# Forming weight low parts by an accumulating DMA in the mLSTM, and turning its last head inside the preceding way down

## The chip, the cores and the metric

The kernel runs on one core of one Trainium2 chip. The metric is the time of one execution on the device, in microseconds; the figure for a kernel is the median of its runs. The core has five engines that run side by side and meet only at semaphores: PE (matrix products), DVE (VectorE), ACT (ScalarE), POOL (GpSimd) and SP, which here only issues DMAs. DMAs issued by SP, ACT and POOL are carried out by the same 16 DMA engines.

## The reference, cut to what matters

Two layers of a streaming encoder over 512 frames of width 1024. Each layer is a half-step SwiGLU FFN, a mixer, a second FFN and a gated embedding, each with a layer norm behind it. The mixer of the first layer is an mLSTM with four heads, and the change lies in it:

```python
def mlstm_mixer(x, w_in, b_in, conv_w, norm_g, w_out):
    proj = x @ w_in + b_in
    qk, v, z, gates = jnp.split(proj, [...], axis=-1)
    qk = jax.nn.silu(causal_depthwise_conv(qk, conv_w))
    ...
    h = mlstm_cell(q, k, v, ig, fg)          # chunked matrix memory, 4 heads of 512 values
    mu = jnp.mean(h, axis=-1, keepdims=True)
    var = jnp.mean(jnp.square(h - mu), axis=-1, keepdims=True)
    h = ((h - mu) * lax.rsqrt(var + LN_EPS)).reshape(B, S, ML_INNER) * norm_g
    h = (h * jax.nn.sigmoid(z)).astype(x.dtype)
    return h @ w_out
```

## The kernel before, in words

All products are float32 built from three products of a narrower type: every operand is split into a high part (the value rounded to that type) and a low part (what the rounding left out), and `mm3` (L252 to L254) adds high times high, high times low and low times high.

**Weights.** The class `Weights` streams all weights through two stages. SP loads 1 MB pieces into a ring of three raw buffers (`wraw`); each gives two tiles of 128x1024. `fill` turns a raw tile into `whi` by a copy on ACT (L182) and `wlo` by a subtraction (L183) on DVE, or on POOL where the caller passes `low=pool`. In the mLSTM there are six tiles of split weights: four of kind "main" and two of kind "extra". A tile is freed by `release`, which fills the next tile of the fixed list `order` if a buffer of that tile's kind is free. With `later=True` the buffer is held until `refill` (which always subtracts on DVE).

**One head.** For each head h the list holds 4 tiles for q and k, 4 for v, 4 for z, and 4 rows of the output weights of the head before. The program order of a head is: `project_qk` (4 groups of 24 matmuls; each group's tile is then released with `low=pool`), `project_v`, `scores`, z blocks 0 and 1, `mix` (the head's values and their norm; a chain of small DVE and POOL operations per block of 128 frames, ending in `hn`), `refill(4)`, z blocks 2 and 3 (released with `low=pool`), and then `down(prev)`: the way down of the head before, 4 blocks of frames t, each 4 row groups k times 6 matmuls (`dps<-whi,hh`, `dps<-wlo,hh`, `dps<-whi,hl`). In the last block each k releases its tile. Then `gate_turn` turns the head's own result: 16 transposes on PE (`hps`, L964), a product with the gate `sz` on DVE (`hzf`, L967), and a split into `hh` on ACT and `hl` on DVE. The next head's way down uses them. After head 3 a last `down` follows at once, with the norm and the transposes of x (`xps`) for the next FFN inside it.

Which kinds the list gives matters at one place: in the way down of head 2, the releases of k = 0 and 1 fill nothing (the next tile is of the other kind), k = 2 fills one tile and k = 3 fills three. The first two of these four are the third and fourth row groups of the last way down, the other two belong to the next FFN.

Each engine works through its instructions in the order written; there is no scheduler.

Of the kernel before, what the change touches and what calls it, by code (L numbers as in the profile page):

```python
# [9 lines left out]
F32 = mybir.dt.float32  # L10
F32R = mybir.dt.float32r
AF = mybir.ActivationFunctionType
OP = mybir.AluOpType
# [3 lines left out]
P = 128  # L17
D = 1024
KB = D // P
SEQ = 512  # L20
TB = SEQ // P
# [3 lines left out]
HEADS = 4  # L25
# [20 lines left out]
class Weights:  # L46
# [112 lines left out]
    def fill(self, most=1000, low=None):  # L159
        while most and self.next_split < len(self.order):  # L160
            kind, js, make = self.order[self.next_split]
            if not self.free.get(kind):
                return
            for j in js or ():
                while j not in self.raws:
                    if not self.load(self.loads[j][1]):
                        return
            shape = [P, 2, 512]
            if js is not None:
                src, used = make()  # L170
                shape = list(src.shape)
            hi = self.pools[kind].tile(shape, F32R, name="whi", tag="whi")
            lo = self.pools[kind].tile(shape, F32R, name="wlo", tag="wlo")
            self.free[kind] -= 1
            self.next_split += 1
            if js is None:
                make(hi, lo)
                continue
            parts = 2 if self.next_split == 1 else 1
            for i in range(parts):  # L180
                s = slice(i * shape[1] // parts, (i + 1) * shape[1] // parts)
                self.nc.scalar.activation(hi[:, s], src[:, s], AF.Copy)  # L182
                (low or self.nc.vector).tensor_sub(lo[:, s], src[:, s], hi[:, s].bitcast(F32))  # L183
            self.ready.append((kind, (hi, lo)))
            most -= 1
            for j in used:
                self.left[j] -= 1
            while self.load():
                pass
# [32 lines left out]
def hybrid_trunk(ctx: ExitStack, tc, x, p, ln_g, ln_b, ffn1_wgu, ffn1_wd, ffn2_wgu, ffn2_wd,  # L222
# [25 lines left out]
    vec, sca, pool = nc.vector, nc.scalar, nc.gpsimd  # L248
# [286 lines left out]
        hooks.extend([lambda: turn_x(TB - 2, halves=(0,)), lambda: turn_x(TB - 2, halves=(1,)),  # L535
                      lambda: turn_x(TB - 1, halves=(0,)), last_turn])

    def down(hs, first, norm=None, low=None):

        n = len(hs)  # L540
        ws, kinds = [], []
        for t in range(TB):
            banks = [dn_bank("dps"), dn_bank("dps")]
            for k in range(n):
                if k == len(ws):
                    ws.append(W.take())
                    kinds.append(W.kind)
                if norm is not None and k in (1, 2) and t >= 2:
                    turn_x(t - 2, up_bank, (k - 1,))
                if norm is not None and k == 1 and t:  # L550
                    norm.apply(t - 1)
                st = [a[:, t * P:(t + 1) * P] for a in hs[k]]
                for half, ps in enumerate(banks):
                    mv = [a[:, 0, half * 512:(half + 1) * 512] for a in ws[k]]
                    mm3(ps, st, mv, k == 0, k == n - 1)
                if t == TB - 1:
                    kind = "rows" if kinds[k] == "rows" else None
                    if norm is None:
                        W.release(kind=kind, low=low)
                    elif kind == "rows":  # L560
                        W.free[kind] += 1
                    else:
                        W.release(later=bool(W.held), low=pool)
                        if not W.held:
                            W.held.append("none")
            for half, ps in enumerate(banks):
                residual(t, half, ps, first)
                if norm is not None:
                    norm.stats(t, half, 2)
        if norm is not None:  # L570
            norm.apply(TB - 1)
            set_hooks()
# [163 lines left out]
    def mlstm():  # L736
        b_in = ml_b_in
        with stage_pool("extra", EXTRA) as extra, stage_pool("ml_parts") as near, stage_pool("ml") as mp:
# [83 lines left out]
            def big(tag, dt, name):  # L822
                return (near if tag in "AB" else mp).tile([P, 4, SEQ], dt, name=name, tag=tag)

            def project_qk(h):

                qh, ql = big("A", F32R, "qh"), big("B", F32R, "ql")

                def project():
                    ps = up_bank("qps")  # L830
                    up(ps, W.take())
                    return ps

                banks = deque()
                if h == 0:
                    banks.extend(up_staged())
                late = None
                for i in range(4):
                    ps = banks.popleft() if banks else project()
                    ch = (i // 2 * QK + h * DQK) // P + i % 2  # L840
                    pad = tmp.tile([P, SEQ + 4], F32, name="pad", tag="pad", bufs=3)
                    vec.memset(pad[:, 0:3], 0.0)
                    sca.activation(pad[:, 3:3 + SEQ], ps, AF.Identity, bias=col("b_qk", ch))
                    acc = tmp_tile("acc")
                    vec.tensor_scalar(acc, pad[:, 0:SEQ], col("conv", ch), None, op0=OP.mult)
                    for j in range(1, CONV):
                        vec.scalar_tensor_tensor(acc, pad[:, j:j + SEQ], col("conv", j * 16 + ch), acc,
                                                 op0=OP.mult, op1=OP.add)
                    if late is not None:
                        late()  # L850

                    def late(i=i, acc=acc):
                        sca.activation(acc, acc, AF.Silu)
                        split(qh[:, i], ql[:, i], acc)

                    W.release(low=pool)
                    if h == 0 and i == 1:
                        gate_products()
                        banks.append(project())
                    run_hook()  # L860
                    if h == 0 and i == 2:
                        gate_logs()
                late()
                return qh, ql
# [18 lines left out]
            def project_z(h, sz, i):  # L883

                ps = up_bank("zps")
                up(ps, W.take())
                sca.activation(sz[:, i], ps, AF.Sigmoid, bias=col("b_z", h * 4 + i))
                vec.tensor_scalar(sz[:, i], sz[:, i], col("norm_g", h * 4 + i), None, op0=OP.mult)
                W.release(later=i < 2, low=pool)

            def row_tile():
                return mp.tile([P, SEQ], F32, name="rbc", tag="rbc")
# [64 lines left out]
                return hn  # L957

            def gate_turn(h, hn, sz):
                hh, hl = big("hh", F32R, "hh"), big("hl", F32R, "hl")  # L960
                for t in range(TB):
                    ps = (dn_bank if t % 2 else up_bank)("hps").rearrange("p (k c) -> p k c", k=4)
                    for i in range(4):
                        nc.tensor.transpose(ps[:, i], hn[:, t, i * P:(i + 1) * P], ident)  # L964
                    s = slice(t * P, (t + 1) * P)
                    hf = tmp_tile("hzf").rearrange("p (k c) -> p k c", k=4)
                    vec.tensor_mul(hf, ps, sz[:, :, s])  # L967
                    split(hh[:, :, s], hl[:, :, s], hf)
                return [(hh[:, i], hl[:, i]) for i in range(4)]

            prev = None
            for h in range(HEADS):
                vb = mp.tile([P, DV], F32, name="vb", tag="sh0")
                sca.dma_start(vb, row_ap(b_in, 2 * QK + h * DV, DV))
                if h:
                    rt = row_tile()
                    load_row(rt, h)
                qk = project_qk(h)
                if h == 0:
                    rt = row_tile()  # L980
                    v = project_v(h, vb, (None, gate_sums, lambda: (gate_rows(), load_row(rt, h))))
                else:
                    v = project_v(h, vb)
                W.release()
                ss = scores(h, qk, rt)
                sz = big("B", F32, "sz")
                W.release()
                W.release(2, later=True)
                for i in range(2):
                    project_z(h, sz, i)  # L990
                hn = mix(h, ss, v)
                W.refill(4)
                for i in range(2, 4):
                    project_z(h, sz, i)
                if prev is not None:
                    down(prev, h == 1, low=pool)
                else:
                    norm = Norm(0, 1)
                prev = gate_turn(h, hn, sz)
            down(prev, False, norm)  # L1000
            W.close("extra")

# [253 lines left out]
```

## Time and profile before

| | |
|---|---|
| median of 3 runs | 2289.18 us (2288.74 to 2290.45) |
| profiled execution, its own time | 2285.76 us |
| its span, first to last instruction | 2284.0 us |
| mean granted PE clock | 0.997 |
| busy: PE, DVE, ACT, POOL | 2239.8, 1495.8, 784.2, 206.4 us |
| mLSTM, about | 366 to 798 us of the span |

In the profile's rows a group is named by the line in the code, the engine, the operation, and output<-inputs by the names of the tiles; then the shape and the count. A row of the timeline begins with its start and its duration in microseconds; what stands in square brackets behind it is how long the engine was idle before it and which engine's work ended that. A row of the waits gives the sum, the number and the longest. A row of the windows gives, for a stretch, its length, each engine's busy time with the number of instructions, the granted PE clock, the mean share of the DMA engines in use, and GB/s.

### The profile page before, as it was taken

Reading aid. Unit: us, or ns where it says so; the run is one execution under the profiler, and the core shown is the slowest. Engines: PE = TensorE matmul, PEld = TensorE weight load, DVE = VectorE, ACT = ScalarE, POOL = GpSimd, SP = SyncE. Lnnn points to the kernel's source line nnn. Section 1 sums busy time; section 2 is a strip of 40 time slices with the busy share of each in tenths; the row PEclk is TensorE's granted clock in tenths of the full one; section 3 lists DMA queues with packets and bytes.
Section 4 is the critical chain, followed back from the end, with each engine's and each line's share of the span. In section 5 each row is a group of like instructions: output and inputs, shape, how many; then the busy total and the mean of one; then the engine's idle time right before and its main releaser. Section 6 shows DMA issues by size and latency. Waiting matters only on the chain.

```text
span 2284.0 us, 26044 instructions
## 1 busy us (share of the span) xinstructions
PE 2239.8 (98%) x10622; PEld 1873.3 (82%) x10622; DVE 1495.8 (65%) x2093; ACT 784.2 (34%) x1032; POOL 206.4 (9%) x143
## 2 busy tenths in 40 slices
PE   8999999999999999999999999999999999999997
PEld 7888888887878788888878888888888888888886
DVE  4566659676666656666687566668566674666677
ACT  3333333442534123333243233333333332333332
POOL 1000002132232300000010000001021210000010
PEclk9999999999999999999999999999999999999999
DMA  7332222133231333331332333222322243332212
GB/s 232 113 98 86 93 86 95 48 114 110 66 102 56 120 111 120 111 96 62 111 120 88 112 105 111 93 70 95 131 93 86 75 133 113 129 111 83 83 65 74
DMA packets 172848, 228.30 MB, mean 100 GB/s; under 512 B 4788, under 2 KB 130836, under 8 KB 172728
## 3 DMA queue, kind: packets, MB, share of 16 engines
q1 hardware_dynamic: 165824, 211.83, 28.6%
q10 hardware_dynamic: 6616, 14.69, 2.0%
q8 instruction: 83, 1.36, 0.2%
q14 instruction: 37, 0.30, 0.0%
q0 software_dynamic: 288, 0.12, 0.0%
HBM read 224.51 MB, written 2.11 MB: 99 GB/s over the span
## 4 chain that ended last, share of the span: by engine, by line
PE 82%; DVE 12%; issue 2%; POOL 2%; ACT 1%; DMA 1%; POOLq 0%; SPq 0%; ACTq 0%; DVEq 0%
PE fps L253 13%; PE fps L254 13%; PE fps L252 13%; PE gps L253 4%; PE gps L254 4%; PE gps L252 4%; PE dps L253 3%; PE dps L254 3%; PE dps L252 3%; DVE wlo L183 2%; DVE xt L512 2%; DVE st L500 1%; PE gups L252 1%; PE vps L252 1%; PE gups L253 1%
## 5 line engine op out<-in xcount | busy, mean ns | idle before, releaser
L252 PE MATMUL fps<-xh,whi 128*128 128x512 f32 x1312 | 510.6, 389 | 0.0
L253 PE MATMUL fps<-xl,whi 128*128 128x512 f32 x1312 | 510.4, 389 | 0.0
L254 PE MATMUL fps<-xh,wlo 128*128 128x512 f32 x1312 | 510.4, 389 | 0.0
L183 DVE TENSOR_TENSOR wlo<-wraw,whi 128x1024 fp32r<-128x1024 f32 (+1 forms) x274 | 336.0, 1242 | 199.2 <-ACT whi L182 197.4
L182 ACT ACTIVATE whi<-wraw 128x1024 fp32r<-128x1024 f32 (+1 forms) x333 | 344.1, 1048 | 263.3 <-PE dps L254 126.2
L252 PEld LDWEIGHTS fps<-xh,whi 128*128 128x128 f32 x1312 | 246.3, 188 | 51.1
L254 PEld LDWEIGHTS fps<-xh,wlo 128*128 128x128 f32 x1312 | 246.3, 188 | 51.0
L253 PEld LDWEIGHTS fps<-xl,whi 128*128 128x128 f32 x1312 | 246.3, 188 | 50.9
L183 DVE TENSOR_TENSOR wlo<-wquarter,whi 128x1024 fp32r<-128x1024 f32 x112 | 137.2, 1225 | 201.9 <-ACT whi L182 201.9
L182 ACT ACTIVATE whi<-wquarter 128x1024 fp32r<-128x1024 f32 x112 | 118.7, 1059 | 238.0 <-PE gps L254 177.8
L183 POOL TENSOR_TENSOR wlo<-wraw,whi 128x1024 fp32r<-128x1024 f32 x59 | 151.8, 2581 | 278.5 <-ACT whi L182 247.4
L254 PE MATMUL gps<-whi,flo 128*128 128x512 f32 x448 | 174.3, 389 | 0.0
L252 PE MATMUL gps<-whi,fhi 128*128 128x512 f32 x448 | 174.3, 389 | 0.0
L253 PE MATMUL gps<-wlo,fhi 128*128 128x512 f32 x448 | 174.3, 389 | 0.0
L508 POOL TENSOR_TENSOR rs<-rs,eps_pow 128x1 f32<-128x1 f32 x32 | 30.3, 947 | 1542.7 <-DVE rs L507 1538.3
L701 ACT ACTIVATE sg<-fps 128x512 f32<-128x512 f32 x80 | 47.9, 598 | 279.1 <-PE fps L254 279.1
L521 DVE TENSOR_TENSOR xt<-xt,gps 128x512 f32<-128x512 f32 x224 | 143.2, 680 | 0.0
L253 PE MATMUL dps<-wlo,hh 128*128 128x512 f32 x256 | 101.6, 397 | 9.5 <-DVE wlo L183 9.5
L257 ACT ACTIVATE fhi<-h 128x512 fp32r<-128x512 f32 x112 | 69.5, 625 | 116.2 <-DVE h L637 45.8
L252 PE MATMUL dps<-whi,hh 128*128 128x512 f32 x256 | 101.9, 398 | 1.8 <-ACT hh L257 1.8
L254 PE MATMUL dps<-whi,hl 128*128 128x512 f32 x256 | 101.4, 396 | 1.7 <-DVE hl L258 1.7
L258 DVE TENSOR_TENSOR flo<-h,fhi 128x512 fp32r<-128x512 f32 x112 | 75.7, 688 | 36.4 <-ACT fhi L257 36.4
(266 smaller groups left out, 3909.6 us busy)
## 6 DMA issues: line engine op xcount, KB each, us to landing
wraw<-in_ffn_wgu_dram SPq DMA_DIRECT2D x80, 1024.0 KB, 5.3
wquarter<-in_ffn_wd_dram SPq DMA_DIRECT2D x64, 512.0 KB, 3.8
wraw<-in_ml_w_in_dram SPq DMA_DIRECT2D x24, 1024.0 KB, 5.4
wraw<-in_gm_w_in_dram SPq DMA_DIRECT2D x15, 1024.0 KB, 5.8
wraw<-in_ffn_wd_dram SPq DMA_DIRECT2D x12, 1024.0 KB, 5.0
wraw<-in_ml_w_out_dram SPq DMA_DIRECT2D x8, 1024.0 KB, 5.0
wraw<-in_ple_wg_dram SPq DMA_DIRECT2D x8, 1024.0 KB, 5.1
wraw<-in_gm_w_out_dram SPq DMA_DIRECT2D x8, 1024.0 KB, 4.9
```

The costliest lines, as they stand in the source:

```text
L182: self.nc.scalar.activation(hi[:, s], src[:, s], AF.Copy)
L183: (low or self.nc.vector).tensor_sub(lo[:, s], src[:, s], hi[:, s].bitcast(F32))
L252: mm(ps, st[0], mv[0], start=start, stop=False, skip_group_check=more)
L253: mm(ps, st[0], mv[1], start=False, stop=False, skip_group_check=more)
L254: mm(ps, st[1], mv[0], start=False, stop=stop, skip_group_check=more)
L257: sca.activation(hi, src, AF.Copy)
L258: vec.tensor_sub(lo, src, hi.bitcast(F32))
L500: vec.bn_stats(self.st[t][:, i], xt[:, t, i * D // n:(i + 1) * D // n])
L508: pool.tensor_tensor(rs[:, 1:2], rs[:, 0:1], eps_pow, op=OP.pow)
L512: vec.scalar_tensor_tensor(y[:, c], y[:, c], rstd, self.b_bc[:, c], op0=OP.mult, op1=OP.add)
L521: vec.tensor_add(dst, dst, ps)
L701: sca.activation(sg, ps, AF.Silu)
```

## The change

Three edits, all in the mLSTM. First, `fill` knows a third way to form a low part, `low="dma"`: ACT writes the negated, rounded value into `wlo` (a second ACT copy per tile), and a DMA issued by POOL adds the raw tile onto it, from SBUF to SBUF. Second, every place in the mLSTM that passed `low=pool` now passes `"dma"`: 36 tiles in all. Third, `gate_turn` returns a function that turns one block of frames; for heads 0 to 2 all four blocks are turned behind the way down as before, and for head 3 each block is turned inside the way down of head 2, behind that way's block t, into buffers that held `vh` and `vl`.

```diff
@@ Weights.fill
                 self.nc.scalar.activation(hi[:, s], src[:, s], AF.Copy)
-                (low or self.nc.vector).tensor_sub(lo[:, s], src[:, s], hi[:, s].bitcast(F32))
+                if low == "dma":
+                    self.nc.scalar.activation(lo[:, s], src[:, s], AF.Copy, scale=-1.0)
+                    self.nc.gpsimd.dma_start(lo[:, s], src[:, s], accum_op=OP.add)
+                else:
+                    (low or self.nc.vector).tensor_sub(lo[:, s], src[:, s], hi[:, s].bitcast(F32))
@@ down
-    def down(hs, first, norm=None, low=None):
+    def down(hs, first, norm=None, low=(None,) * 4, between=None):
...
-                        W.release(kind=kind, low=low)
+                        W.release(kind=kind, low=low[k])
...
                 residual(t, half, ps, first)
...
+            if between is not None:
+                between(t)
@@ mlstm, project_qk and project_z
-                    W.release(low=pool)
+                    W.release(low="dma")
...
-                W.release(later=i < 2, low=pool)
+                W.release(later=i < 2, low="dma")
@@ gate_turn
-                hh, hl = big("hh", F32R, "hh"), big("hl", F32R, "hl")
-                for t in range(TB):
-                    ps = (dn_bank if t % 2 else up_bank)("hps").rearrange("p (k c) -> p k c", k=4)
+                if h < HEADS - 1:
+                    hh, hl = big("hh", F32R, "hh"), big("hl", F32R, "hl")
+                else:
+                    hh, hl = (near.tile([P, 4, SEQ], F32R, name=n, tag=g) for n, g in (("hh", "vh"), ("hl", "vl")))
+                def turn(t):
+                    ps = (dn_bank if t % 2 and h < HEADS - 1 else up_bank)("hps").rearrange("p (k c) -> p k c", k=4)
...
-                return [(hh[:, i], hl[:, i]) for i in range(4)]
+                return [(hh[:, i], hl[:, i]) for i in range(4)], turn
@@ the loop over heads
+                last = h == HEADS - 1
+                if last:
+                    hs, turn = gate_turn(h, hn, sz)
                 if prev is not None:
-                    down(prev, h == 1, low=pool)
+                    down(prev, h == 1, low=[None, None, "dma", "dma"] if last else ["dma"] * 4,
+                         between=turn if last else None)
...
-                prev = gate_turn(h, hn, sz)
+                if not last:
+                    hs, turn = gate_turn(h, hn, sz)
+                    for t in range(TB):
+                        turn(t)
+                prev = hs
```

What stands on ACT at the way down of head 2 and into the last one (whi and wlo are tiles of split weights, hh the turned result of head 3, xh the turned x for the next FFN). Before:

```order
L182 ACTIVATE whi_6002<-wraw_5822 128x1024
L182 ACTIVATE whi_6012<-wraw_5822 128x1024
L182 ACTIVATE whi_6018<-wraw_5832 128x1024
L182 ACTIVATE whi_6024<-wraw_5896 128x1024
L257 ACTIVATE hh<-hzf 128x4x128 x4
```

And in the changed kernel:

```order
L262 ACTIVATE hh_5930<-hzf_6039 128x4x128
L182 ACTIVATE whi_6063<-wraw_5852 128x1024
L185 ACTIVATE wlo_6064<-wraw_5852 128x1024
L182 ACTIVATE whi_6074<-wraw_5852 128x1024
L185 ACTIVATE wlo_6075<-wraw_5852 128x1024
L182 ACTIVATE whi_6081<-wraw_5862 128x1024
L185 ACTIVATE wlo_6082<-wraw_5862 128x1024
L182 ACTIVATE whi_6088<-wraw_5928 128x1024
L185 ACTIVATE wlo_6089<-wraw_5928 128x1024
L262 ACTIVATE hh_5930<-hzf_6102 128x4x128
```

Each of the four tiles now takes two ACT copies, and three of the four splits of the turned blocks stand ahead of them instead of behind.

What stands on POOL from the end of head 3's `mix` on (hr is the norm of the last blocks). Before:

```order
L952 TENSOR_TENSOR hr<-hr,eps_pow 128x1 x4
L183 TENSOR_TENSOR wlo<-wraw,whi 128x1024 x6
L508 TENSOR_TENSOR rs<-rs,eps_pow 128x1 x2
```

And in the changed kernel:

```order
L959 TENSOR_TENSOR hr_5829<-hr_5829,eps_pow_105 128x1
L186 DMA wlo_5892<-wraw_5659 128x1024
L186 DMA wlo_5924<-wraw_5659 128x1024
L186 DMA wlo_6064<-wraw_5852 128x1024
L186 DMA wlo_6075<-wraw_5852 128x1024
L186 DMA wlo_6082<-wraw_5862 128x1024
L186 DMA wlo_6089<-wraw_5928 128x1024
L513 TENSOR_TENSOR rs_6147<-rs_6147,eps_pow_105 128x1
```

Six subtractions became six issues of a DMA, at the same places in POOL's order.

What stands on PE at the join between the two ways down. Before:

```order
L254 MATMUL dps<-whi,hl 128x512
L964 MATMUL hps<-ident,hn 128x128 x16
L252 MATMUL dps<-whi,hh 128x512
```

And in the changed kernel, where such a group of four stands behind each of the four blocks (the last is shown):

```order
L259 MATMUL dps<-whi,hl 128x512
L977 MATMUL hps<-ident,hn 128x128 x4
L257 MATMUL dps<-whi,hh 128x512
```

Twelve of the sixteen transposes moved ahead, into the way down of head 2; four are left at the join.

## The prediction

> **What bounds the kernel now.** I read the page's first part, then PE's waits, then windows over the ways down of the mLSTM, and last the timeline around each wait.
>
> ```profile
> PE 2239.8 (98%) x10622; PEld 1873.3 (82%) x10622; DVE 1495.8 (65%) x2093; ACT 784.2 (34%) x1032; POOL 206.4 (9%) x143
> PE dps L253 <- DVE wlo L183: 9.5, 6, 1.8
> 533.06:559.48 26.42, 22.93 (x97) 17.83 (x96) 13.14 (x16) 4.82 (x5) 5.26 (x3) 1.00 0.35 120
> 637.60:663.49 25.89, 22.91 (x97) 17.83 (x96) 12.93 (x15) 4.82 (x5) 6.14 (x3) 1.00 0.36 122
> 741.61:767.52 25.91, 22.92 (x98) 17.82 (x97) 12.94 (x15) 2.69 (x3) 3.35 (x2) 1.00 0.28 82
> 767.52:798.10 30.58, 27.94 (x129) 22.47 (x128) 24.96 (x40) 8.71 (x12) 14.98 (x8) 0.94 0.44 155
> 761.42 1.39 DVE L521 TENSOR_TENSOR xt<-xt,dps 128x512 f32<-128x512 f32 x2 [4.21 <-PE dps L254]
> 767.02 1.39 DVE L521 TENSOR_TENSOR xt<-xt,dps 128x512 f32<-128x512 f32 x2 [4.21 <-PE dps L254]
> ```
>
> PE is busy 98% of the span, and the change removes no matmul: it can only win where PE stands still. PE waits for a DVE low part six times, all in the ways down. The four windows are the three ways down inside heads 1 to 3 and the last one. The two residual rows, 5.60 us apart, give the undisturbed pace: one block of 24 matmuls in 5.60, a way down in 22.40, one k of six in 1.40, one matmul in 0.233. The three ways take 78.22 instead of 67.2: 11.0 us lost.
>
> Why DVE is late there:
>
> ```profile
> 530.66 2.40 POOL L183 TENSOR_TENSOR wlo<-wraw,whi 128x1024 fp32r<-128x1024 f32 x1
> 530.73 2.35 DVE L953 TENSOR_TENSOR hr<-hr 128x1 f32<-128x1 f32 x1 [0.73 <-POOL hr L952]
> 534.02 4.54 DVE L183 TENSOR_TENSOR wlo<-wraw,whi 128x1024 fp32r<-128x1024 f32 x2
> 535.02 2.45 POOL L183 TENSOR_TENSOR wlo<-wraw,whi 128x1024 fp32r<-128x1024 f32 x1 [1.97 <-ACT whi L182]
> 533.06 0.39 PE L252 MATMUL dps<-whi,hh 128*128 128x512 f32 x1
> 535.29 0.50 PE L253 MATMUL dps<-wlo,hh 128*128 128x512 f32 x1 [1.84 <-DVE wlo L183]
> 538.61 0.50 PE L253 MATMUL dps<-wlo,hh 128*128 128x512 f32 x1 [1.65 <-DVE wlo L183]
> L953 DVE TENSOR_TENSOR hr<-hr x16: 159/160/2359, 441.3 to 739.0; 128x1 f32<-128x1 f32 x16
> L183 DVE TENSOR_TENSOR wlo<-wraw,whi x274: 681/1224/3418, 7.9 to 2237.2; 128x1024 fp32r<-128x1024 f32 x136, 128x512 fp32r<-128x512 f32 x1
> ```
>
> A DVE operation on one column, median 0.16 us, takes 2.35 and ends with POOL's subtraction; the next pair takes 4.54 instead of 2 times 1.22 beside another. While POOL subtracts, DVE stands. The two hits are 2.2 and 2.1 us, and PE's two waits follow.
>
> **The change, part by part.** *POOL's 36 subtractions go.* Without the first hit the first low part is there at 535.29 − 2.2 = 533.1; PE wants it one matmul after 533.06, at 533.29. Without both, the second is there at 538.61 − 4.3 = 534.3, wanted 1.40 after the first, at 534.7. Both waits go, by 0.2 and 0.4 us. Taken over three heads: 11.0 gained. The DMA that replaces the first subtraction is issued at the same moment, and I know one row for an issue of as many pieces (1024):
>
> ```profile
> 5.18 0.95 POOL L469 DMA_DIRECT2D graw<-in_ml_w_in_dram  x1
> ```
>
> DVE was idle there, so whether an issue holds DVE is not shown. If it does, DVE loses 0.8 of the 2.2 us, 0.6 past its margin, in three heads: 9.2 is the lower end, 11.0 the upper. I take 11.0, since the page shows DVE held by arithmetic of POOL alone.
>
> *The last head's turn moves.* Now PE stands behind the 16 transposes:
>
> ```profile
> 767.52 1.91 PE L964 MATMUL hps<-ident,hn 128*128 128x128 f32 x16
> 771.24 0.50 PE L252 MATMUL dps<-whi,hh 128*128 128x512 f32 x1 [1.82 <-ACT hh L257]
> 772.80 0.70 PE L254 MATMUL dps<-whi,hl 128*128 128x512 f32 x1 [0.82 <-DVE hl L258]
> 769.40:772.90 3.50, 0.86 (x4) 0.40 (x3) 1.68 (x2) 1.79 (x3) 3.50 (x3) 1.00 0.00 0
> 772.90:776.30 3.40, 3.40 (x9) 2.66 (x10) 2.54 (x3) 0.76 (x2) 3.40 (x2) 0.50 0.88 284
> 766.32 1.06 ACT L182 ACTIVATE whi<-wraw 128x1024 fp32r<-128x1024 f32 x1 [22.88 <-PE dps L254]
> ```
>
> It waits 1.82 and 0.82, and after that thin stretch the granted clock is 0.50 for 3.40 us, which costs 1.7: 4.3 in all. With the turns inside the way down of head 2, three blocks are split long before and the fourth is wanted only 17 us later: the 4.3 come back. The transposes themselves (1.91) stay.
>
> *But the third and fourth row groups of the last way down now get their low parts by DMA.* Call X the time from POOL's issue to landing, and T = 767.52 the end of the way down of head 2. ACT starts the third group's `whi` at T − 1.20 (row 766.32); two copies of 1.06 end at T + 0.92, the data are there at T + 0.92 + X. PE wants them after 4 transposes (0.48), two k (2.80) and one matmul (0.23): T + 3.51. Wait: X − 2.6. The fourth group's two copies follow on ACT and end 2.12 later, PE wants it 1.40 later: 0.7 more. Together X − 1.9, and likely the half clock again (1.7).
>
> *How long is X?* No accumulating DMA is in the trace.
>
> ```profile
> wquarter<-in_ffn_wd_dram SPq DMA_DIRECT2D x64, 512.0 KB, 3.8
> wraw<-in_ml_w_out_dram SPq DMA_DIRECT2D x8, 1024.0 KB, 5.0
> prow<-in_ml_conv_dram POOLq DMA_DIRECT2D x1, 32.0 KB, 4.7
> graw<-in_ml_w_in_dram POOLq DMA_DIRECT2D x1, 32.0 KB, 6.9
> ```
>
> Another 512 KB costs 1.2 (5.0 − 3.8), and a POOL-issued DMA with hardly any data takes 4.7 to 6.9. The tile is 512 KB, read from two places. From below: 3.8, a plain load. Near: 4.7 + 2 × 1.2 = 7.1. From above, adding slower than copying: 6.9 + 5.0, about 12. I take 7, since POOL's queue is the nearest row. Then the last way down loses 5.1 + 1.7 = 6.8 where it lost 4.3: −2.5.
>
> The Trainium skill (DMA: Bandwidth & Descriptors, section "Anatomy of one DMA — SWDGE (gpsimd) path") gives about 2.0 us plus bytes over 436 GB/s for a DMA issued by GpSimd. By it an estimate for 512 KB read twice is 4.4, and the sum would gain 12.8; the two 32 KB rows stand far above its 2.1, so the trace does not agree so far.
>
> *The other 34 tiles.* The nearest deadline is the fourth tile of v, filled when the second q, k group is released:
>
> ```profile
> 456.62 0.48 PE L252 MATMUL qps<-xh,whi 128*128 128x512 f32 x1
> 478.50 0.39 PE L252 MATMUL vps<-whi,xh 128*128 128x512 f32 x1
> 478.42 1.05 ACT L182 ACTIVATE whi<-wraw 128x1024 fp32r<-128x1024 f32 x1
> 687.05 0.39 PE L252 MATMUL vps<-whi,xh 128*128 128x512 f32 x1
> 682.84 1.04 ACT L182 ACTIVATE whi<-wraw 128x1024 fp32r<-128x1024 f32 x1
> 680.34 1.28 ACT L853 ACT_TABLE_LOAD   x1 [3.28 <-DVE pad L842]
> 471.48 4.36 DVE L847 SCALAR_TENSOR_TENSOR acc<-pad,cols,acc 128x512 f32<-128x512 f32 x3
> 476.49 2.33 DVE L847 SCALAR_TENSOR_TENSOR acc<-pad,cols,acc 128x512 f32<-128x512 f32 x3
> 459.52 3.04 DVE L888 TENSOR_SCALAR sz<-sz,cols 128x512 f32<-128x512 f32 x2
> 540.75 0.87 DVE L888 TENSOR_SCALAR sz<-sz,cols 128x512 f32<-128x512 f32 x2
> 460.00:570.00 110.00, 106.51 (x510) 88.95 (x509) 75.32 (x124) 42.05 (x65) 31.02 (x19) 1.00 0.32 104
> ```
>
> 96 matmuls from 456.62 to 478.50 are 0.228 each; the tile's low part is wanted 19 later: 482.83 in head 1, 691.38 in head 3. ACT's `whi` for it waits for the convolution on DVE, which gets faster (4.36 becomes 2.33). In head 3 the whi thus starts some 1.7 earlier than 682.84 (the copies added ahead hide in 3.28 us of idle ACT), and the DMA is issued 2.1 later, at 683.2: 8.2 us to spare. In head 1 the hits of 2.2 (one column), 2.2 (`sz`) and 2.0 (convolution) all go: issue at 478.42 − 6.4 + 2.1 = 474.1, 8.7 to spare. X = 7 is hidden, by one microsecond. The remaining tiles are wanted 15 us or more after their release, hidden under whole groups of matmuls of 5.5 each.
>
> *What else is lengthened.* ACT gets 36 copies of 1.05, 38 us, at 42 busy of 110 in head 1: nothing waits but the DMAs counted above. POOL's queue: behind the DMA issues stand the four masks and norm steps of the next `mix`, due 10 us later or more; nothing. SP: a raw buffer is freed at landing, some 5.5 us later than now (1.05 + 7 − 2.5), and the ring holds six tiles, so a load of 5.0 is still early: nothing.
>
> **Sum.** 11.0 − 2.5 = 8.5. The profiled execution's own 2285.76 would become 2277.3; on the median of 2289.18, which lies 3.4 above it, that is 2280.7. I forecast 2280.5.
>
> **The rivals.** In X the gain is 15.5 − X up to 8.2, and past that three v tiles wait as well: 15.5 − X − 3 (X − 8.2).
> - *The landing is slow (the other side).* Place: the fourth v tile in heads 1 to 3. From X = 10.0 on the kernel loses; at 12 it is 2289.2 + 7.9 = 2297. For it: nothing here shows how fast a DMA adds. Against: 10 is twice a 1 MB load.
> - *It comes out even:* X of 8.9 to 11.2 leaves the change within 4.6 us, about 2289.
> - *The landing is quick:* the data hide behind POOL's fixed time, X = 4.7. The wait is 2.8, too short for the half clock: 11.0 + 4.3 − 2.8 = 12.5, 2276.7. At the lower end, 3.8, it is 2275.8. Against: the two POOL rows are from queues that hold other loads, but moved hardly any data.
> - *The change doesn't free DVE:* the issue holds DVE as the subtraction did. Then the six waits stay, the last way down costs 2.5, and in head 1 the v tile comes at 480.5 + 7 for 482.83, 4.7 late: 2296. For it: the issue stands at the very place. Against: 0.95 is less than half of 2.40. The Trainium skill (same page, section "SWDGE vs HWDGE vs iDMA") says that GpSimd writes a DMA's descriptors into SBUF, and that VectorE can lock it out of that; no run here shows it yet.
>
> **How the numbers follow.** Chances: forecast (X of 5 to 8.9) 0.52, quick 0.15, even 0.12, slow 0.13, DVE held 0.08. About 0.2% (4.6 us) is what a measurement of this kernel can tell from no change. Faster: 0.52 + 0.15 = 0.67; slower: 0.13 and most of the held case, 0.19; the rest 0.14. Range: from the quick case at its lower end less what the fastest run lies under the median (0.4), 2275, to the held case, 2296, which takes in most of the slow one; some 0.1 to 0.15, above all slow landings of 12 and more, stay outside.
>
> **What would show it.** Right: no wait of `dps` for a DVE `wlo` in heads 1 to 3 and ways down of 22.4 to 23; `hr` at L953's successor at 0.16 throughout; one wait of about 5 us at the third row group of the last way down, for a DMA, with the clock at 0.50 behind it; landings near 7. Wrong: waits of `vps` for a DMA (slow landing), a DVE operation as long as a DMA issue (DVE held), or a last way down without a wait (quick).

## The result, and the profile after

| | before | after |
|---|---|---|
| median | 2288.96 us (4 runs, 2284.99 to 2290.45) | 2275.15 us (4 runs, 2274.01 to 2275.3) |
| ratio | | 0.994, 95% interval 0.9928 to 0.9952 |
| profiled execution, its own time | 2285.76 us | 2275.0 us |

The change gains 13.8 us by the medians, 10.8 between the two profiled executions. The forecast was a gain of 8.5. The range holds the time by 0.15 us, and the case that came nearest is a rival: the quick landing (2276.7).

First the page's busy line, after:

```profile
PE 2239.6 (99%) x10622; PEld 1875.5 (83%) x10622; DVE 1440.3 (63%) x2093; ACT 816.8 (36%) x1068; POOL 151.1 (7%) x143
```

PE's waits from 350 to 850 us of the span, after (the one for `xl` is at 371 us):

```profile
PE dps L258 <- DMA wlo<-wraw: 3.3, 2, 2.1
PE sup L603 <- DVE xl L425: 2.4, 1, 2.4
```

The row `dps <- DVE wlo` (9.5 us, six times) is gone. DVE is busy 55 us less, though it does the same 2093 instructions: that time was never work. The windows over the same four ways down (the third now holds twelve of the transposes, which add 1.3 us: 23.71 for 22.39):

```profile
534.21:556.60 22.39, 22.39 (x98) 17.98 (x96) 9.14 (x12) 6.58 (x8) 3.30 (x2) 1.00 0.83 187
635.00:657.39 22.39, 22.39 (x97) 17.98 (x96) 9.50 (x12) 6.58 (x8) 3.08 (x2) 1.00 0.84 188
735.51:759.22 23.71, 23.71 (x110) 19.17 (x109) 12.70 (x18) 5.64 (x8) 0.86 (x1) 1.00 0.48 125
759.22:787.61 28.39, 25.05 (x118) 19.86 (x116) 19.41 (x35) 10.40 (x13) 8.76 (x8) 1.00 0.75 186
```

In the first three PE never stands: 22.39 is the pace that the prediction took from undisturbed blocks. The four together went from 108.80 to 96.88, 11.9 less. What is left of waiting stands in the last one (PE's timeline there, after):

```profile
764.95 0.50 PE L258 MATMUL dps<-wlo,hh 128*128 128x512 f32 x1 [2.12 <-DMA wlo<-wraw]
767.83 0.50 PE L258 MATMUL dps<-wlo,hh 128*128 128x512 f32 x1 [1.22 <-DMA wlo<-wraw]
```

POOL's timeline, with the issues of these two tiles:

```profile
760.36 0.85 POOL L186 DMA_DIRECT2D wlo<-wraw  x1 [20.91 <-DVE xt L526]
762.26 0.86 POOL L186 DMA_DIRECT2D wlo<-wraw  x1 [1.04 <-ACT wlo L185]
```

The landing time of the first of them, taken alone:

```profile
DMA to landing us min/median/max: 4.5/4.5/4.5
```

And the page's row of all 36 (KB each, median us to landing):

```profile
wlo<-wraw POOLq DMA_DIRECT2D x36, 512.0 KB, 7.4
```

The first tile that PE waits for lands 4.5 us after its issue and the second 5.5, while the median over all 36 is 7.4.

And the clock, which moved too. Windows around three places before; the granted clock is the third figure from the end:

```profile
360.00:376.00 16.00, 13.58 (x94) 12.34 (x93) 14.85 (x23) 3.46 (x5) 4.34 (x3) 1.00 0.28 82
760.00:780.00 20.00, 17.36 (x75) 13.72 (x75) 10.03 (x12) 6.43 (x8) 10.28 (x4) 0.91 0.35 111
1210.00:1235.00 25.00, 20.90 (x163) 20.70 (x162) 20.35 (x37) 7.43 (x14) 4.24 (x3) 0.93 0.20 64
```

The same after:

```profile
360.00:376.00 16.00, 13.58 (x80) 12.27 (x79) 14.80 (x23) 2.96 (x5) 4.34 (x3) 0.89 0.26 82
760.00:780.00 20.00, 16.66 (x76) 12.92 (x75) 11.62 (x22) 7.47 (x10) 5.41 (x6) 1.00 0.96 221
1210.00:1235.00 25.00, 21.05 (x133) 19.93 (x132) 16.93 (x25) 11.37 (x15) 0.92 (x1) 0.86 0.39 129
```

0.91 of 20 us and 0.93 of 25 are one piece of 3.4 us at half clock each, 0.86 of 25 are two. After, there is none in the last way down, but one at 371 us, where both kernels wait the same 2.4 us, and two instead of one at 1214. Each piece costs 1.7 us, and they fall differently in each execution. The profiled execution before is itself 3.2 us under its kernel's median, the one after 0.2; such pieces can account for the 10.8 of the pair beside the 13.8 of the medians, but only the profiled executions show where they fall.

### The profile page after: what moved, and what is told of

It reads as the page before. It is cut to its first block, busy times and chain, and to the rows that moved or that the text cites. A ratio compares the mean times of both kernels' runs of the same rounds, so it can differ in the third digit from the quotient of the medians.

```text
span 2273.3 us, 26142 instructions
## 1 busy us (share of the span) xinstructions
PE 2239.6 (99%) x10622; PEld 1875.5 (83%) x10622; DVE 1440.3 (63%) x2093; ACT 816.8 (36%) x1068; POOL 151.1 (7%) x143
## 3 DMA queue, kind: packets, MB, share of 16 engines
q1 hardware_dynamic: 165824, 211.83, 28.5%
## 4 chain that ended last, share of the span: by engine, by line
PE 86%; DVE 9%; ACT 1%; issue 1%; POOL 1%; DMA 1%; POOLq 0%; SPq 0%; ACTq 0%
PE fps L258 13%; PE fps L257 13%; PE fps L259 13%; PE gps L258 4%; PE gps L257 4%; PE gps L259 4%; PE dps L258 3%; PE dps L259 3%; PE dps L257 3%; DVE xt L517 2%; DVE st L505 1%; PE gups L257 1%; PE vps L257 1%; PE vps L258 1%; PE zps L257 1%; DVE wlo L188 1%
## 5 line engine op out<-in xcount | busy, mean ns | idle before, releaser
L188 DVE TENSOR_TENSOR wlo<-wraw,whi 128x1024 fp32r<-128x1024 f32 (+1 forms) x274 | 329.4, 1218 | 199.2 <-ACT whi L182 197.4
L257 PEld LDWEIGHTS gps<-whi,fhi 128*128 128x128 f32 x448 | 84.1, 188 | 17.5
```

The lines of the kernel that those rows point to most:

```text
L257: mm(ps, st[0], mv[0], start=start, stop=False, skip_group_check=more)
```

## The experiments

### Who has to subtract

All 36 by DVE, the turn moved as in the change:

```diff
-                    W.release(low="dma")
+                    W.release()
...
-                down(prev, h == 1, low=[None, None, "dma", "dma"] if last else ["dma"] * 4,
+                down(prev, h == 1, low=[None] * 4,
```

> The changed kernel, but all 36 low parts are DVE's subtractions (27 + 36 of them in the mLSTM, 1.22 us each, 44 us more of DVE), no DMA and no second ACT copy. Theory 1 (what was gained in the ways down is POOL no longer holding DVE; who subtracts else hardly matters): the ways down stay at 22.4, the two waits for a DMA in the last one (3.3 us) go: 2275.2 - 3.3 = 2271.9. Theory 2 (the DMA is needed, because DVE works in order and stands still for ACT's whi while convolution and residuals queue behind): the wait moves to the fourth v tile and to the low parts of the ways down, 1.5 to 2 us a head and more: 2277 to 2283.

Measured: 2271.05 us (0.9927, 0.9915 to 0.994). The page's busy line, and PE's waits from 350 to 850:

```profile
PE 2236.8 (99%) x10622; PEld 1873.1 (83%) x10622; DVE 1479.5 (65%) x2129; ACT 784.5 (35%) x1032; POOL 111.4 (5%) x107
PE sup L603 <- DVE xl L425: 4.2, 2, 2.4
```

The windows over the third and the last way down (the first two take 22.40 each):

```profile
735.97:759.69 23.72, 23.72 (x109) 19.17 (x108) 14.34 (x20) 4.59 (x6) 0.00 (x0) 1.00 0.28 89
759.69:784.75 25.06, 24.88 (x118) 19.86 (x117) 22.91 (x36) 6.94 (x9) 4.50 (x3) 1.00 0.37 126
```

Theory 1 holds. With 36 more subtractions on DVE no low part is late: what made them late was POOL's arithmetic, and the DMA is not needed to end it. DVE is even busy 16 us less than before (1479.5 for 1495.8), with 36 instructions more. The last way down takes 25.06, the 3.3 us are gone; 1.8 of them return right behind, as a second wait for `xl`.

Only the four tiles released in head 2's way down by DVE, 32 left to the DMA (`low=[None] * 4 if last else ["dma"] * 4`):

> The changed kernel with DVE subtracting the four tiles released in head 2's way down, two of which are the third and fourth row groups of the last way down; 32 tiles stay with the DMA. Theory 1 (the 3.3 us of waits there are the DMA's landing and nothing else): both waits go, the last way down takes 25.1 instead of 28.4 us, 2275.2 - 3.3 = 2271.9. Theory 2 (the next thing is late right behind it: ACT's whi, or the turned block hl, which now stands behind the subtractions on DVE): 1 us or less is gained, 2274.5.

Measured: 2272.08 us (0.9929, 0.9917 to 0.9942), the last way down 25.07: theory 1, with the same second wait for `xl`. The DMA is hidden for the other 32.

### What the turn is worth, and to which kernel

The turn moved, POOL still subtracting (`"dma"` replaced by `pool` in the changed kernel):

> POOL still subtracts; only the last head's turn is moved into the way down of head 2. My theory: the two parts of the change act in different places, so this gives back only the 4.3 us of the join (waits of 1.82 and 0.82 and half a clock window of 3.4 us): about 2284.7 against 2289.0, ways down of head 0 to 2 still 25.9 to 26.4 us. The third and fourth row groups come from POOL in time, by 0.1 us for the fourth. Rival: the turned blocks put two DVE operations per block into a way down in which POOL holds DVE, and PE waits for a residual or for the low part instead: 2287 or more.

Measured: 2285.22 us against 2288.34 (0.9983, 0.9974 to 0.9991), 3.1 gained. The first, third and last ways down:

```profile
536.58:565.11 28.53, 25.35 (x98) 19.44 (x96) 13.14 (x16) 4.82 (x5) 5.25 (x3) 0.88 0.32 111
747.24:774.45 27.21, 24.23 (x110) 19.01 (x109) 16.82 (x21) 4.59 (x6) 3.34 (x1) 1.00 0.25 78
774.45:799.10 24.65, 24.65 (x118) 19.95 (x116) 20.78 (x34) 6.83 (x9) 14.71 (x8) 1.00 0.37 128
```

Third and last together 51.86 instead of 56.49: 4.6 back, as theory 1 said. The first way down shows what its two waits may cost besides: 6.8 us at half clock lie around and behind them here (0.88 of 28.5 us), where the kernel before, with the same waits, had none (1.00). Of the 11 runs, three with a mean clock of 0.997 took 2281.4 to 2283.3, the eight with 0.994 or 0.995 took 2284.8 to 2286.7.

The DMA alone, the turn as before:

> The 36 low parts come from the accumulating DMA, the last head is turned behind the way down of head 2 as before. Theory 1 (the two parts depend on each other, through ACT's queue): the ways down are 22.4 us, 11.0 gained, but four more ACT copies of about 0.96 us stand ahead of the first turned block, so the wait of 1.82 us for hh grows to about 5.2 and one clock window is lost as before: 2289.0 - 11.0 + 3.4 = 2281.4, and no wait for a DMA. Theory 2 (the parts simply add): 11.0 gained and the join as before: 2278.0.

Measured: 2278.95 us (0.9961, 0.9947 to 0.9975): 9.4 gained, between the 7.6 and the 11.0 of the theories. PE's timeline at the join:

```profile
766.22 0.80 PE L257 MATMUL dps<-whi,hh 128*128 128x512 f32 x1 [5.15 <-ACT hh L262]
```

The windows over the third and the last way down:

```profile
736.77:759.16 22.39, 22.39 (x98) 17.98 (x96) 8.82 (x12) 3.79 (x5) 0.87 (x1) 1.00 0.50 132
759.16:791.84 32.68, 27.53 (x130) 22.41 (x129) 23.27 (x41) 12.24 (x16) 8.78 (x8) 0.95 0.79 209
```

The mechanism of theory 1 is there, 5.15 for the expected 5.2: the second ACT copies stand ahead of the turned block. But the way is only 2.1 longer than before (30.58), not 3.4, because the later wait for `hl` (0.82) goes with it and PE is busy 0.4 us less (27.53 for 27.94). The time by itself doesn't tell the theories apart; the row does.

DVE alone, the turn as before (the kernel before without its three `low=pool`):

> The kernel before with all 36 low parts subtracted by DVE instead of POOL, nothing else: three small edits. Theory 1 (the turn at the join then queues behind the subtractions on DVE): the ways down are 22.4, 11.0 gained, but the first turned block comes only after the fourth subtraction, about 2 us later than now, so the wait for hh is 3.8 and 9.0 are gained: 2279.3 against 2288.3; the turn moved ahead is then worth 8 us, since the kernel with both took 2271.05. Theory 2 (the parts add without touching each other): 2277.3.

Measured: 2278.66 us (0.9955, 0.9943 to 0.9968). PE's wait at the join, then the third and the last way down:

```profile
PE dps L252 <- ACT hh L257: 5.4, 1, 5.4
736.70:759.10 22.40, 22.40 (x97) 18.00 (x96) 10.51 (x14) 2.70 (x3) 0.00 (x0) 1.00 0.30 95
759.10:793.30 34.20, 28.81 (x129) 23.35 (x128) 28.26 (x45) 8.81 (x12) 5.34 (x4) 0.90 0.40 138
```

The time lies between the theories' 2279.3 and 2277.3, and its interval holds both; the row decides for theory 1, with a wait for `hh` of 5.4 where 3.8 was expected. So the turn is worth, on the two ways down that it touches in the profiled executions, 4.6 us in POOL's kernel (56.49 to 51.86), 3.0 in the DMA's (55.07 to 52.10, since it uncovers the wait for the landing) and 7.8 in DVE's (56.60 to 48.78): both cures of the ways down put more work ahead of the old turn. Half clock is in these figures, 1.7 us in the first two and 3.4 in the third (0.90 of 34.2 us). By the medians, each gain taken against its own kernel before, the turn is worth 3.1, 4.4 and 7.6: only DVE's stands apart.

### The landing time

Half of each tile by the DMA, half by DVE:

> The changed kernel, with the DMA adding only the first half of each of the 36 tiles, 256 KB, and DVE subtracting the other half (0.61 us). Looked at for the landing times alone. Theory 1 (a fixed time of issue and start makes up most of the landing): the lone tile of the last way down lands after about 4.0 us instead of 4.5, the loaded ones after 6 to 10 instead of 8 to 12.8. Theory 2 (the bytes make up most): 3.2 instead of 4.5 and the loaded ones half, 4 to 6.5, and the two waits of the last way down (2.1 and 1.2 us) all but vanish.

The page's row of the 36 issues:

```profile
wlo<-wraw POOLq DMA_DIRECT2D x36, 256.0 KB, 4.7
```

The landing of the first of the two tiles in the last way down:

```profile
DMA to landing us min/median/max: 3.3/3.3/3.3
```

What PE waits for them:

```profile
PE dps L264 <- DMA wlo<-wraw: 0.6, 2, 0.5
```

Theory 2 holds for the lone tile: the bytes make up more than half. 512 KB take 4.5, 256 KB 3.3, so an estimate from these two landings is 2.4 us for the tile's bytes and 2.1 that don't depend on them. The second tile took 3.7 instead of 5.5. The waits fall from 3.3 to 0.6, in part because ACT's second copy, of half a tile, takes 0.62 instead of 1.04 and the issues come earlier. The one run took 2272.2.

Each tile added twice:

```diff
-                    self.nc.scalar.activation(lo[:, s], src[:, s], AF.Copy, scale=-1.0)
-                    self.nc.gpsimd.dma_start(lo[:, s], src[:, s], accum_op=OP.add)
+                    self.nc.scalar.activation(lo[:, s], src[:, s], AF.Copy, scale=-2.0)
+                    for _ in range(2):
+                        self.nc.gpsimd.dma_start(lo[:, s], src[:, s], accum_op=OP.add)
```

> The changed kernel with the cost in dispute doubled: ACT writes -2 times the rounded value and the raw tile is added twice, by two DMAs one behind the other, so that each tile takes about twice as long to land (and the low parts are twice their size, which makes the result less exact). Lone tiles land 4.5 us after their issue now, so about 9.5; the v tile 5.5 to 9.3, so about 14. Theory 1 (the slack that the prediction worked out holds: the fourth v tile has 8.2 to 8.7 us): it is 5 to 6 us late in three heads, 16 together; the last way down waits some 8 us more than 3.3 for its two row groups: 2275.2 + 24 = 2299, with waits of vps for the DMA. Theory 2 (the tiles have far more slack, only the last way down feels the landing): 2283, no wait of vps.

Measured: 2376.08 us (1.0381, 1.0367 to 1.0395), 100 over the changed kernel where 24 was the most expected. PE's waits for the DMA:

```profile
PE vps L259 <- DMA wlo<-wraw: 48.3, 11, 6.6
PE qps L260 <- DMA wlo<-wraw: 13.2, 2, 6.6
PE dps L259 <- DMA wlo<-wraw: 11.4, 2, 6.9
```

What POOL stood still for ahead of its issues (us, times; the first row of the list):

```profile
  DMA wlo<-wraw: 313.9, 54
```

Both theories miss: the second addition waits on POOL for the first to land, and every later tile's issue queues behind that, 314 us of standing in all. It shows what a wait in POOL's queue does, not where the landing's slack ends; adding twice doubles the latency only by closing the queue. How far X could grow was not settled.

### Where DVE's own room ends

The 23 subtractions that POOL does outside the mLSTM, on DVE too:

> The kernel with all 36 on DVE and the turn moved (2271.05), and now also the 23 subtractions that POOL still does outside the mLSTM put on DVE. Theory 1 (POOL's subtractions cost only where PE stands behind DVE, and outside the mLSTM it hardly does): no change, 2270 to 2272. Theory 2 (the waits of gps for low parts, 2.3 us in four, and the 1.3 and 0.9 of the gMLP come from POOL holding DVE too): 2267.5 to 2268.7.

Measured: 2277.06 us (0.9951, 0.9937 to 0.9964): slower than with those on POOL (2271.05, and 2272.94 in the last comparison below), and neither theory. The three medians are from three chips, against kernels before within 0.7 us of each other; the interval here overlaps the other two a little, so the size of the loss is uncertain. PE's waits that grew, over the whole span:

```profile
PE xps L422 <- DVE xt L517: 5.3, 3, 4.3
PE dps L257 <- ACT hh L262: 2.5, 2, 1.5
```

2.5 us for `hh` in the gMLP are new, and the `xl` wait behind the last way down is 2.9 instead of 1.7. Of the 3.6 us between the two profiled executions all waits together are 2.1; the second also has two more pieces at half clock, more than the rest needs, so the rest is not told apart. It suggests that where DVE is the next to be late, POOL's 2.4 us are cheaper than DVE's 1.2 in DVE's queue.

Last, one spot done three ways on one chip: the two FFN tiles released at the end of head 2's way down, by DVE, DMA or POOL, with the other 34 on DVE.

```diff
-                down(prev, h == 1, low=[None] * 4,
+                down(prev, h == 1, low=[None, None, None, [None, "dma", "dma"]] if last else [None] * 4,
```

(`fill` takes the list's entries tile by tile; with `pool` in place of `"dma"` in the second kernel.)

> The kernel with all 36 on DVE and the turn moved, but the two tiles of the next FFN that are released at the end of head 2's way down come from the DMA. With all on DVE, DVE has no gap from 764.5 to 789 us, and PE then waits 1.74 us for xl. Theory 1 (DVE's backlog there begins with the four subtractions): 2.4 us less of it, the wait of 1.74 goes, 2271.05 - 1.7 = 2269.3. Theory 2 (the norm's own chain sets that wait): no change.

> The same two tiles subtracted by POOL (2.4 us each) instead. Theory 1 (DVE stands for the whole of POOL's subtraction): DVE loses 4.8 where it lost 2.4 with its own subtractions, the wait for xl becomes about 4.1, 2273.5. Theory 2 (POOL's work only slows single DVE operations, the total is less than DVE's own 2.4): the wait shrinks, 2270 or less.

> The changed kernel again, beside the others on one chip: 13 to 14 us under the kernel before.

> All 36 on DVE and the turn moved again, beside the changed kernel on one chip. Theory 1 (the DMA costs what it waits in the last way down, 3.3 us, less the 1.8 that return at xl, give or take a clock window of 1.7): 1.5 to 4 us faster than the changed kernel. Theory 2 (the earlier gap came from another chip): the same.

| on one chip, before 2288.98 us | median | ratio |
|---|---|---|
| the changed kernel (e11) | 2274.63 | 0.9936 (0.9922 to 0.9949) |
| all on DVE, turn moved (e12) | 2272.94 | 0.9933 (0.9921 to 0.9945) |
| the two tiles by DMA (e9) | 2270.70 | 0.9920 (0.9906 to 0.9933) |
| the two tiles by POOL (e10) | 2273.35 | 0.9932 (0.9919 to 0.9944) |

The four intervals overlap, so the order rests on the profiles. The changed kernel gained 14.4 where 13 to 14 was expected. All on DVE is 1.7 faster than it: inside the 1.5 to 4 of theory 1, but the runs of the two overlap (2271.95 to 2274.77 against 2271.51 to 2276.07), so theory 2 is not excluded by the times. The wait for `xl` with two tiles by DMA:

```profile
PE sup L604 <- DVE xl L426: 3.0, 2, 2.4
```

Two tiles by DMA leave 3.0 us of waits for `xl` where the all-DVE kernel has 4.2: theory 1, though 0.6 of the wait stays. Its ratio is the lowest of the study, but not apart from those of the all-DVE kernels. With POOL the row is 4.2 again, of which 2.4 are at another place: the wait is 1.8, as with DVE's own subtractions, not the 4.1 of theory 1 and not less. That the time is near theory 1's 2273.5 is no proof of it. POOL's timeline there:

```profile
762.64 4.86 POOL L189 TENSOR_TENSOR wlo<-wraw,whi 128x1024 fp32r<-128x1024 f32 x2 [28.45 <-ACT whi L183]
```

And DVE's:

```profile
762.79 1.28 DVE L527 TENSOR_TENSOR xt<-xt,dps 128x512 f32<-128x512 f32 x2
763.99 0.68 DVE L981 TENSOR_TENSOR hzf<-hps,sz 128x512 f32<-128x512 f32 x1
765.37 2.68 DVE L264 TENSOR_TENSOR hl<-hzf,hh 128x512 fp32r<-128x512 f32 x1 [0.70 <-ACT hh L263]
```

Three DVE operations take no longer than their usual 0.69 each beside POOL, and only the fourth is held, for 2.0 us. The three read a bank of matmul results (`dps`, `hps`), the fourth reads two SBUF tiles.

## Why the prediction was right or wrong

- **Three ways down, +11.0: right.** 78.22 became 68.49 with 1.3 us of moved transposes in it: 11.05. The mechanism holds, since DVE's subtraction instead of the DMA's brings the same 22.4.
- **"While POOL subtracts, DVE stands": too wide.** It holds DVE operations that take their operands from SBUF. Groups of the mLSTM before (count: shortest/median/longest in ns; two SBUF operands, one SBUF operand with a column, then two kinds that read matmul results):

```profile
L258 DVE TENSOR_TENSOR ql<-acc,qh x16: 678/690/2891, 390.6 to 698.2; 128x512 fp32r<-128x512 f32 x16
L888 DVE TENSOR_SCALAR sz<-sz,cols x14: 473/482/2643, 459.5 to 749.5; 128x512 f32<-128x512 f32 x14
L967 DVE TENSOR_TENSOR hzf<-hps,sz x13: 677/684/692, 462.7 to 768.3; 128x512 f32<-128x512 f32 x13
L521 DVE TENSOR_TENSOR xt<-xt,dps x16: 686/686/690, 646.2 to 767.7; 128x512 f32<-128x512 f32 x16
```

After, without POOL's subtractions, the first two again, and the single column `hr`, whose longest was 2359 before (what is left above the median lies beside DMA issues, see the next point):

```profile
L263 DVE TENSOR_TENSOR ql<-acc,qh x16: 683/684/817, 390.4 to 690.5; 128x512 fp32r<-128x512 f32 x16
L895 DVE TENSOR_SCALAR sz<-sz,cols x14: 480/486/918, 459.2 to 739.2; 128x512 f32<-128x512 f32 x14
L960 DVE TENSOR_TENSOR hr<-hr x16: 159/159/160, 443.1 to 733.2; 128x1 f32<-128x1 f32 x16
```

  It did no harm to the sum, since the operations hit in the ways down were SBUF ones. The Trainium skill (SBUF — State Buffer, section "Who interferes with whom") says that VectorE and GpSimd share one pair of ports, taken by DVE instructions with two SBUF inputs or in a two-port mode, not by one with at most one SBUF input otherwise. These rows agree with it, if `sz` runs in such a mode, which no row shows.
- **The rival that an issue holds DVE as the subtraction did: wrong.** `hr` runs beside three issues, one of which starts at the same 531.87 as it, and takes 0.16 each time. But an issue is not free: it lengthened other DVE operations, above all those on one SBUF operand with a column, by up to 0.7 us a pair. After (the pair of `sz` takes 0.87 undisturbed, row 540.75 before):

```profile
537.51 1.20 DVE L895 TENSOR_SCALAR sz<-sz,cols 128x512 f32<-128x512 f32 x2
638.08 1.55 POOL L186 DMA_DIRECT2D wlo<-wraw  x1 [3.85 <-ACT wlo L185]
638.32 1.56 DVE L895 TENSOR_SCALAR sz<-sz,cols 128x512 f32<-128x512 f32 x2
```

  No `dps` wait for a DVE low part came of it; the ways down stay at 22.39.
- **The last way down, −2.5: the step that failed.** It was to lose 6.8 and lost 3.3 (2.12 + 1.22) where it had lost 4.3: +1.0. Two terms were mis-sized. X was taken as 7 and is 4.5 and 5.5 for these two tiles; and the half clock (1.7), which was to follow the wait, did not come. The rows for X, two loads of 32 KB from DRAM at 4.7 and 6.9, were from the program's start and no model of a transfer in SBUF; the quick rival's "Against" knew that other loads stood in those queues, and it was given too little weight. That the half clock stayed away is no proof of the rival's "too short": at 371 us a wait of 2.4 was followed by it after and not before. The sign named for the rival, a last way down without a wait, did not fit its own sum, which had 2.8; 3.3 was waited. The range held the time by luck: its lower end came from an X of 3.8, which no whole tile showed. The estimate of 4.4 from the Trainium skill (DMA: Bandwidth & Descriptors, "Anatomy of one DMA — SWDGE (gpsimd) path"), set aside there, is close to the first lone tile (4.5, and 3.3 for half the bytes against 3.2 by the same rule); the second tile's 5.5 and the median of 7.4 lie above it.
- **The fourth v tile, "hidden, by one microsecond": right where it was worked out.** In heads 1 and 3 the landing took 5.5 and 7.5 and nothing waited. Head 2 was not worked out; there it took 7.9, the load of that tile's weights into PE waited 0.4, and PE lost 0.3. Landings run from 4.5 to 12.8, so the 7 is near the middle of all 36 (median 7.4) and wrong for the two that PE waits for.
- **ACT's 36 copies at nothing: right only because the turn moved.** Without it they cost 3.3 us at `hh` (5.15 against 1.82). The prediction priced the two parts side by side and did not see that one covers the other.
- **The rest.** In the profiled pair the last way down ends 10.5 us earlier (787.61 for 798.10): 11.9 on the four ways, less 1.15 lost ahead of the first (the piece at 371 alone costs 1.7) and 0.3 between the first two (the v tile). Behind it another 0.2 is gained: the `xl` waits fall by 1.0, from the following row before to the 2.4 shown above,

```profile
PE sup L596 <- DVE xl L420: 3.4, 2, 2.4
```

  and the second piece at 1214 takes 1.7 back, which leaves 0.9 unassigned. Why the medians differ by 13.8 is not traced further.

## What to carry to other kernels

Before a faster path is bought for work on an idle engine, ask what that engine does to its neighbours: here the plain DVE subtraction, half as long as POOL's, gave the same ways down as the DMA without its landing time, wherever DVE had room. A DMA's landing is to be priced by its bytes and by who else is on the queues at that place, and only the tile with the least time to its use counts. Two parts of a change that meet in one engine's queue are worth what they are worth together: the turn was worth 3 to 5 us where POOL or the DMA forms the low parts and 8 where DVE does.

## What the runs showed of the hardware that was not expected

An addition by DMA takes more of the DMA engines than a load: from 366 to 800 us after, the two queues moved (megabytes, share of the 16 engines' time)

```profile
q0 software_dynamic: 19520, 18.88, 30.6%
q1 hardware_dynamic: 25152, 35.13, 24.5%
```

so a megabyte added took 2.3 times the engines' time of a megabyte loaded, and median loads of `wraw` from `w_in` rose from 5.4 to 5.9 us. The issue itself takes POOL 0.85 to 0.93 us for the two v tiles first issued (one piece of 4 KB in each partition) and 1.54 and 1.56 for the z tiles behind them (eight pieces of 512 bytes). One issue of eight pieces took 1.82, beside the pair of `sz` operations that took 1.20 in place of 0.87.
